# The last expert pass of a hybrid decoder block: its 128 places summed, normed and stored by index, and all tokens' rows stored under its products

## The chip, the cores and the metric

The kernel runs on one core of a Trainium2 chip. The metric is device time in microseconds (us) of one execution; a lower number is better. Three runs of the kernel before took 749.69, 751.23 and 755.02 us, so its median is 751.23 us. The profiled execution is a run of its own. It took 751.85 us, of which 750.1 us lie between its first and its last instruction (the span); the other 1.75 us lie outside.

A core has five engines with instruction streams of their own: PE (matrix products), DVE (vector), ACT (scalar functions), POOL and SP (here it only starts transfers). Each works through its stream in order and waits on semaphores.

## The reference, cut to what matters

One layer: a token mixer, then a mixture of experts, each in a residual branch, and a last RMS norm. There are 512 tokens of 1024 features. The change touches only how the experts' results are added to `x` and how the last norm and the output are made.

```python
def rms_norm(x, w):
    y = x * lax.rsqrt(jnp.mean(x * x, axis=-1, keepdims=True) + EPS)
    return y * w

def hier_moe(h, ...):            # 512 tokens, 32 experts, each token uses 2 experts of one group
    ...                          # comb[t, group, expert]: the two weights of a token, else 0
    for gi in range(N_GROUPS):
        a = silu(t @ w_e_gate[gi]) * (t @ w_e_up[gi])
        y = y + einsum('tef,te,efd->td', a, comb[:, gi], w_e_down[gi])
    return y

x = x + g1 * token_mixer(...)
h = rms_norm(x, norm2_w) * (1 + sc2) + sh2
x = x + g2 * hier_moe(h, ...)
return rms_norm(x, final_norm_w)
```

## The kernel before, in words

The experts are computed in 13 passes (`PASSES`, numbers 0 to 12; `NP` is 13). A pass has 128 **places**, shared out among two or four experts. The last pass has four experts (26 to 29) with 32 places each. A place holds one token of its expert, or is empty. `meta[:, 1]` is the place's token number, and `idx` the same as an integer. An empty place has a number of 512 or more, so that a transfer by index skips it.

One pass does this:

1. `up` multiplies the places' rows by the gate and up weights into the bank `gu`, in eight blocks `k`; blocks 0 to 3 use one set of weight tiles, blocks 4 to 7 another. With four experts each block is four products of 32 columns, which stand in four column groups of the PE array and can run beside each other. Between the two halves PE does the `add`s of the pass before (below).
2. ACT takes the silu of the gate half (line 1749), DVE multiplies it by the up half and the place's weight (`gate`, line 1754), PE turns the result (`turn`, line 1762) and ACT copies it out (line 1763).
3. `down` multiplies by the experts' down weights into two banks, one for each half of the features, and DVE scales them by g2 into `yf` (line 1784). In the last pass the products of the last expert, whose weights come last, stand behind those of the other three.
4. `add` returns the places' rows to their tokens: a 0/1 matrix `oht` (places by tokens) times `yf`, as a high and a low part (`yhi` from ACT, line 1785; `ylo` from DVE, line 1786), for 8 pieces of 128 tokens by 512 features. DVE adds each piece to `acc`, where the tokens' rows of `x` lie (line 1800).

After the last pass there is no later pass to hide the adds, so the kernel before does them another way. `total` (line 1429) puts each of the 8 pieces of `acc` into a bank with a product by the identity; these 8 products stand in the last pass where PE has gaps. After `down`, `add` adds the last pass's rows on top in the same banks (lines 1797, 1798). Then, token block by token block, ACT squares and sums the row (`squares`, line 1434), DVE makes the inverse root (`rsqrt`, lines 154 to 157, with a root on ACT, line 153), DVE, ACT and POOL scale by it and by the norm's weight (`finish`, lines 1449 to 1452) and SP stores the block of 128 rows (line 1453). Behind that, ACT and DVE copy all 8 banks back to `acc` (lines 1499, 1501), because `rest`, the program for tokens that don't fit into the places, would need them there; with this input no token is left over, and `rest` is branched past.

In the last pass `warm` also issues 12 and 8 small products by the identity, ahead of each half of `up` (line 1735, which calls line 215); nothing uses their results.

The order on PE and SP is that of the program text: each `step` holds its instructions behind the PE and SP instructions of the step before. The weights come as tiles of 1 MB through SP's queue (`load`, lines 974 and 976); the transfer of a tile waits for the eighth transfer before it to have landed, by one of eight semaphores in turn, and for its buffer to be free.

## Time and profile before

| | us |
|---|---|
| median of three runs | 751.23 |
| the profiled execution | 751.85 |
| its span | 750.1 |
| PE, DVE, ACT, POOL busy | 710.3, 510.5, 283.2, 91.3 |

The last passes and the end, by stretches of the span:

| stretch, us | what | PE busy | DVE busy | ACT busy | GB/s |
|---|---|---|---|---|---|
| 690.0 to 701.2 | pass 11 | 11.18 | 7.44 | 2.16 | 418 |
| 701.2 to 712.3 | pass 12, first half of `up`, adds of pass 11 | 11.15 | 5.09 | 2.23 | 419 |
| 712.3 to 730.7 | pass 12, second half of `up`, `down` | 18.37 | 3.33 | 2.88 | 222 |
| 730.7 to 750.1 | adds of pass 12, norm, stores, copies | 6.16 | 13.32 | 10.18 | 111 |

Up to 730.7 PE is busy all the time by this table, but it counts the small products of `warm` and the products by the identity too. So whether PE sets the pace in a stretch is read from what starts when, not from the share. From 730.7 on it is DVE and ACT, and then the last store.

### The profile page before, as it was taken

The numbers are of one execution on the slowest core, as the hardware profiler recorded it, in microseconds if no ns is written. First come the engines' busy times: TensorE is split into PE (matmuls) and PEld (weight loads), VectorE is DVE, ScalarE is ACT, GpSimd is POOL, SyncE is SP. The second block draws the span as 40 slices with busy tenths as digits, with TensorE's granted clock in tenths as the row PEclk, the third lists the DMA queues.
The fourth block names the chain that finished last, engine by engine and source line by source line (L and its number), as shares of the span: only waits on it lengthen the run. The fifth ranks groups of instructions, "written<-read, shape, count | busy, mean of one in ns | idle before, by whom it ended". The sixth has DMA issues, their size and how long they took to land.

```text
span 750.1 us, 11135 instructions
## 1 busy us (share of the span) xinstructions
PE 710.3 (95%) x4000; PEld 487.8 (65%) x4000; DVE 510.5 (68%) x1247; ACT 283.2 (38%) x548; POOL 91.3 (12%) x72
## 2 busy tenths in 40 slices
PE   7789999999998989999999999999999999999992
PEld 6567768878786868886768877884444444444631
DVE  5997678978646666768867744277776677766516
ACT  4345436852233212556753233224222322222215
POOL 1863000320222200000000000010100000000002
PEclk9999999999999999999999999999999999999997
DMA  9833223028787741361147997267999999999952
GB/s 360 301 129 115 84 88 108 30 66 297 240 279 244 240 165 57 99 239 49 58 148 283 342 422 291 78 254 261 403 408 403 403 411 411 410 412 419 419 211 114
DMA packets 47373, 182.89 MB, mean 244 GB/s; under 512 B 11717, under 2 KB 13285, under 8 KB 33875
## 3 DMA queue, kind: packets, MB, share of 16 engines
q1 hardware_dynamic: 40690, 169.91, 60.4%
q10 hardware_dynamic: 4896, 8.25, 3.0%
q0 software_dynamic: 1728, 3.99, 1.4%
q8 instruction: 32, 0.52, 0.3%
q14 instruction: 27, 0.21, 0.1%
HBM read 175.63 MB, written 8.80 MB: 246 GB/s over the span
## 4 chain that ended last, share of the span: by engine, by line
PE 71%; DVE 13%; DMA 8%; ACT 4%; issue 3%; POOL 0%; SPq 0%; DVEq 0%; ACTq 0%; POOLq 0%
PE gu L1726 12%; PE pj L139 9%; PE pj L141 9%; PE pj L140 9%; PE cb L1780 7%; DMA sgF<-w_mod 6%; PE cb L1797 3%; PE cb L1798 3%; DVE sF L220 3%; DVE sgF L220 2%; PE ax L801 2%; PE tr L1647 2%; DVE uS L145 1%; DMA aF<-rl 1%; DVE sh L315 1%
## 5 line engine op out<-in xcount | busy, mean ns | idle before, releaser
L139 PE MATMUL pj<-hR,uR 128*128 128x512 f32 x304 | 121.9, 401 | 1.5 <-DVE qk L737 1.5
L141 PE MATMUL pj<-hR,uS 128*128 128x512 f32 x304 | 122.1, 401 | 1.1 <-DVE uS L145 1.1
L140 PE MATMUL pj<-hR,uR 128*128 128x512 f32 x304 | 121.5, 400 | 0.0
L144 ACT ACTIVATE uR<-uF 128x1024 fp32r<-128x1024 f32 x48 | 50.8, 1059 | 92.3 <-PE pj L140 81.5
L145 DVE TENSOR_TENSOR uS<-uF,uR 128x1024 fp32r<-128x1024 f32 x48 | 59.7, 1243 | 24.6 <-ACT uR L144 24.2
L1800 DVE TENSOR_TENSOR accF<-accF,cb 128x512 f32<-128x512 f32 x96 | 60.3, 681 | 22.2 <-PE cb L1798 21.1
L1726 PE MATMUL gu<-ra,uS 128*64 128x512 f32 (+1 forms) x344 | 70.0, 597 | 0.0
L141 PEld LDWEIGHTS pj<-hR,uS 128*128 128x128 f32 x304 | 57.6, 189 | 13.4 <-DVE uS L145 3.2
L139 PEld LDWEIGHTS pj<-hR,uR 128*128 128x128 f32 x304 | 57.4, 189 | 12.5 <-issue 2.7
L140 PEld LDWEIGHTS pj<-hR,uR 128*128 128x128 f32 x304 | 57.5, 189 | 10.5 <-issue 0.3
L220 DVE SCALAR_TENSOR_TENSOR sgF<-sgF,misc 128x1024 f32<-128x1024 f32 x32 | 39.5, 1239 | 20.2 <-DMA sgF<-w_mod 19.9
L1726 PEld LDWEIGHTS gu<-ra,uS 128*64 128x64 f32 (+1 forms) x344 | 19.3, 123 | 36.4 <-issue 35.6
L1797 PE MATMUL cb<-uR,oht 128*128 128x512 f32 x100 | 42.6, 426 | 0.0
L1785 ACT ACTIVATE uR<-p2F 128x512 fp32r<-128x512 f32 x26 | 16.3, 630 | 65.9 <-DVE p2F L1784 65.9
L1749 ACT ACTIVATE uS<-gu 128x256 f32<-128x256 f32 x13 | 5.0, 384 | 95.7 <-PE gu L1726 95.7
L1798 PE MATMUL cb<-uR,oht 128*128 128x512 f32 x100 | 39.5, 395 | 0.1
L1780 PE MATMUL cb<-ra,uS 128*32 128x512 f32 (+1 forms) x160 | 38.3, 597 | 0.1
L1612 POOL DMA_INDIRECT uF<-xd,idx x12 | 12.4, 1036 | 180.1 <-PE tr L1647 121.6
L1754 DVE SCALAR_TENSOR_TENSOR uS<-uS,meta,gu 128x256 f32<-128x256 f32 x13 | 6.2, 481 | 37.1 <-ACT uS L1749 37.1
L1726 PE MATMUL gu<-rb,uS 128*32 128x512 f32 (+1 forms) x184 | 29.1, 595 | 0.0
L1784 DVE TENSOR_TENSOR p2F<-cb,p2F 128x512 f32<-128x512 f32 x26 | 17.8, 687 | 15.6 <-PE cb L1780 15.6
L220 DVE SCALAR_TENSOR_TENSOR sF<-sF,misc 128x1024 f32<-128x1024 f32 x16 | 27.7, 1740 | 0.2 <-DMA sF<-w_mod 0.2
(455 smaller groups left out, 1500.0 us busy)
## 6 DMA issues: line engine op xcount, KB each, us to landing
ra<-w_e SPq DMA_DIRECT2D x55, 1024.0 KB, 9.3
rb<-w_e SPq DMA_DIRECT2D x25, 1024.0 KB, 10.0
uF<-w_in SPq DMA_DIRECT2D x38, 512.0 KB, 3.5
sgF<-w_mod SPq DMA_DIRECT2D x32, 512.0 KB, 4.5
rc<-w_e SPq DMA_DIRECT2D x15, 1024.0 KB, 9.7
sF<-w_mod SPq DMA_DIRECT2D x8, 1024.0 KB, 9.5
gd<-sgF ACTq DMA_DIRECT2D x16, 256.0 KB, 3.6
gF<-gd SPq DMA_DIRECT2D x8, 512.0 KB, 3.6
```

The lines of the kernel that those rows point to most:

```text
L139: mm(ps, whi, xhi, start=first, stop=False)
L140: mm(ps, whi, xlo, start=False, stop=False)
L141: mm(ps, wlo, xhi, start=False, stop=last)
L144: self.nc.scalar.activation(hi, raw, AF.Copy)
L145: self.nc.vector.tensor_sub(lo, raw, hi.bitcast(F32))
L220: self.nc.vector.scalar_tensor_tensor(raw, raw, 1.0, self.cact, op0=OP.mult, op1=OP.mult, accum_out=self.mod[:, ot:ot + 1])
L1726: nc.tensor.matmul(gu[r], xe[:, k, r], w[:, k % 4], start=k == 0, stop=k == 7)
L1780: nc.tensor.matmul(dn[h][r], aT[:, f, r], w[:, f, c], start=f == 0, stop=f == 1)
L1784: v.tensor_mul(self.yf[:, c], dn[h], self.g2r[:, c])
L1797: nc.tensor.matmul(pc, self.oht[:, ts], self.yhi[:, c], start=own, stop=False)
L1798: nc.tensor.matmul(pc, self.oht[:, ts], self.ylo[:, c], start=False, stop=True)
L1800: nc.vector.tensor_add(self.acc[:, t, c], self.acc[:, t, c], pc)
```

## The change

The last pass's rows no longer go back to all 512 tokens. Instead:

- `alike` makes `same`, a 128 by 128 matrix that has a 1 where two places hold the same token, and a float copy `ohf` of the pass's matrix of tokens by places.
- `gather(h)` multiplies the tokens' rows in `acc` (with passes 0 to 11 added) by `ohf` into one bank for each half of the features: 4 products each. The bank then holds, for each place, its token's row. `gather(0)` stands between the halves of `up`, `gather(1)` behind `up`.
- All 512 tokens' rows are normed and stored during the last pass as they are then: `squares` on ACT, `roots` on DVE and ACT, `finish(0)` ahead of `gate` on DVE, `finish(1)` to `finish(3)` behind it; POOL no longer takes part. Tokens that have no place in the last pass are finished by that.
- After `down`, `finish_last` adds `same` times `yf` to the gathered rows (one product for each half), ACT squares and sums, DVE multiplies by the norm's weight, `store_last` makes the inverse root, scales the rows on ACT and DVE and stores the 128 rows by index, over those stored before. POOL issues this store, and waits for the four plain stores first.
- `warm` in the last pass, `total`, the 8 last adds, their high and low part, and the copies back are gone. The adds that `rest` needs stand inside its branch.

```diff
@@ moe: the last pass
             if p == NP - 1:
                 self.step(self.finish_init)
+                with ExitStack() as late:
+                    for x in self.after_down:
+                        late.enter_context(tc.issue_after(x))
+                    self.step(self.alike, p)
             self.up(p, p > 0, between=self.first_steps if p == 0 else None)
...
-                with tc.issue_after(self.sil.ins):
-                    nc.scalar.activation(self.rs[:, 0:1], self.ones[:, 0:1], AF.Sqrt)
+                self.step(self.gather, 1)
...
+            self.step(self.turn, p)
             if p == NP - 1:
-                self.dns = [self.bank() for _ in range(2)]
-                self.totals(2)
-            self.step(self.turn, p)
+                with tc.issue_after(self.gated.ins):
+                    for t in range(1, 4):
+                        self.finish(t)
+                with tc.issue_after(self.turned.ins):
+                    nc.scalar.activation(self.nt[:, 0:1], self.ones[:, 0:1], AF.Sqrt)
...
+            self.step(self.down, p, PASSES[p])
             if p == NP - 1:
-                self.totals(2)
-            self.step(self.down, p, PASSES[p])
+                for h in range(2):
+                    self.step(self.finish_last, h)
+                self.store_last(p)
...
-        for n in range(8):
...
-            self.step(self.add, n, self.fin[n])
-            self.squares(t, h, self.fin[n])
-            if h:
-                self.finish(t, (self.fin[n - 1], self.fin[n]))
@@ up
-            if p == NP - 1 and k % 4 == 0:
-                self.step(self.warm, self.bank(), self.ident, WL[k // 4])
             self.step(block, k)
...
             if p == NP - 1:
                 if k == 3:
                     for n in range(8):
                         self.step(self.add, n)
-                    self.totals(1)
+                    self.step(self.gather, 0)
+                    for ts in ((0, 1), (2, 3)):
+                        self.squares(ts)
+                        self.roots(ts)
+                    self.finish(0)
@@ new functions
+    def alike(self, p):
+        nc, tok = self.nc, self.meta[p % 4][:, 1:2]
+        nc.scalar.activation(self.ohf, self.oh[p % 2].rearrange("p t s -> p (t s)"), AF.Copy)
+        pr = self.tr.tile([128, 512], F32, name="tr")
+        nc.tensor.transpose(pr[:, 0:128], tok.to_broadcast([128, 128]), self.ident)
+        nc.vector.tensor_scalar(self.same, pr[:, 0:128], tok, None, op0=OP.is_equal)
+    def gather(self, h):
+        g = self.fin[h] = self.bank()
+        for t in range(4):
+            self.nc.tensor.matmul(g, self.ohf[:, 128 * t:128 * t + 128], self.half(2 * t + h), start=t == 0, stop=False)
+    def finish(self, t):
+        o = self.rows_out[t]
+        for h in range(2):
+            self.nc.vector.scalar_tensor_tensor(o[:, 512 * h:512 * h + 512], self.half(2 * t + h), self.rs[:, t:t + 1],
+                                                self.fw[:, 512 * h:512 * h + 512], op0=OP.mult, op1=OP.mult)
+        self.nc.sync.dma_start(self.out[t * 128:(t + 1) * 128], o)
+    def finish_last(self, h):
+        nc, v, o = self.nc, self.nc.vector, self.ends
+        c = slice(512 * h, 512 * h + 512)
+        s, g = self.ss[:, h, 4:5], self.fin[h]
+        nc.tensor.matmul(g, self.same, self.yf[:, c], start=False, stop=True)
+        nc.scalar.activation(self.sqj[2 + h], g, AF.Square, accum_out=s)
+        v.tensor_mul(o[:, c], g, self.fw[:, c])
+        if h == 0:
+            v.tensor_scalar(s, s, 1.0 / D, EPS, op0=OP.mult, op1=OP.add)
+    def store_last(self, p):
...
+        nc.scalar.activation(rs, s1, AF.Sqrt, scale=1.0 / D, bias=s0)
+        v.scalar_tensor_tensor(s1, s1, 1.0 / D, s0, op0=OP.mult, op1=OP.add)
+        self.rsqrt(rs, s1, "4", self.nt[:, 4:5], root=False)
+        nc.scalar.activation(o[:, 0:512], o[:, 0:512], AF.Copy, scale=rs)
+        v.tensor_scalar(o[:, 512:], o[:, 512:], rs, None, op0=OP.mult)
+        nc.gpsimd.indirect_dma_start(out=self.out, out_offset=bass.IndirectOffsetOnAxis(ap=self.idx[p % 4][:, :1], axis=0),
+                                     in_=o, in_offset=None, bounds_check=511, oob_is_err=False)
```

Where the instructions stand now, at three places. First PE between the two halves of `up` of the last pass. `cb` and `gu` are banks, `uR` the high and low rows, `ct` the identity, `rc` and `ra` weight tiles, and `rb_3430` holds `ohf`. Before, and then with the change:

```order
L1797 MATMUL cb<-uR,oht 128x512
L1798 MATMUL cb<-uR,oht 128x512
L1429 MATMUL gu<-accF,ct 128x512
L215 MATMUL cb<-ct 128x128 x8
L1726 MATMUL gu<-rc_3929,uS 32x512
L1726 MATMUL gu<-rc_3928,uS 32x512
```

```order
L1822 MATMUL cb<-uR,oht 128x512
L1823 MATMUL cb<-uR,oht 128x512
L1434 MATMUL cb<-accF,rb_3430 128x512 x4
L1750 MATMUL gu<-rc_3929,uS 32x512
L1750 MATMUL gu<-rc_3928,uS 32x512
```

One product by the identity and 8 small ones are replaced with the 4 products of `gather(0)`.

Second, PE in `down` of the last pass, from its second row on (`ra_3102` to `ra_3104` are the down weights of the first three experts, `rb_3427` those of the last). Before, and then with the change:

```order
L1780 MATMUL cb<-ra_3103,uS 32x512
L1780 MATMUL cb<-ra_3102,uS 32x512
L1780 MATMUL cb<-ra_3103,uS 32x512
L1429 MATMUL gu<-accF,ct 128x512
L1780 MATMUL cb<-ra_3104,uS 32x512
L1780 MATMUL cb<-ra_3102,uS 32x512
L1780 MATMUL cb<-ra_3103,uS 32x512
L1780 MATMUL cb<-ra_3104,uS 32x512 x2
L1780 MATMUL cb<-ra_3102,uS 32x512
L1780 MATMUL cb<-ra_3103,uS 32x512
L1780 MATMUL cb<-ra_3104,uS 32x512
L1780 MATMUL cb<-rb_3427,uS 32x512 x4
```

```order
L1807 MATMUL cb<-ra_3103,uS 32x512
L1807 MATMUL cb<-ra_3102,uS 32x512
L1807 MATMUL cb<-ra_3104,uS 32x512
L1807 MATMUL cb<-ra_3102,uS 32x512
L1807 MATMUL cb<-ra_3103,uS 32x512
L1807 MATMUL cb<-ra_3104,uS 32x512
L1807 MATMUL cb<-ra_3103,uS 32x512
L1807 MATMUL cb<-ra_3104,uS 32x512
L1807 MATMUL cb<-ra_3102,uS 32x512
L1807 MATMUL cb<-ra_3103,uS 32x512
L1807 MATMUL cb<-ra_3104,uS 32x512
L1807 MATMUL cb<-rb_3427,uS 32x512 x4
```

The product by the identity no longer stands between the third expert's products and those of the first two.

Third, ACT from the start of the last pass to its last row (line 1441 is `squares`, 152 the root, 1775 the silu, 1789 the copy of `turn`, 1465 to 1477 the end). With the change:

```order
L1425 ACTIVATE rb_3430<-uS 128x512
L1441 ACTIVATE rb_3431,ss_5991<-accF 128x512 x8
L152 ACT_TABLE_LOAD
L152 ACTIVATE rs_5992<-ss_5991 128x2 x2
L1775 ACT_TABLE_LOAD
L1775 ACTIVATE uS<-gu 128x256
L1789 ACTIVATE uS<-tr 128x256
L1388 ACT_TABLE_LOAD
L1388 ACTIVATE nt_5993<-ct 128x1
L1465 ACTIVATE rb_3431,ss_5991<-cb 128x512 x2
L1474 ACTIVATE rs_5992<-ss_5991 128x1
L1477 ACTIVATE rb_3430<-rb_3430,rs_5992 128x512
```

Before, the silu (line 1749) was ACT's first instruction of the pass behind the copies of line 1464, and one table load stood behind it; now 8 squares, two roots and two table loads stand ahead of it, and one load behind the copy of `turn`.

## Rows read from the trace of the kernel before

**Rows 1.** Timeline, PE, last pass: start us, length us, engine, line, operation, count.

```profile
704.88 0.63 PE L1726 MATMUL gu<-ra,uS 128*32 128x512 f32 x3
...
712.33 1.02 PE L1429 MATMUL gu<-accF,ct 128*128 128x512 f32 x2
713.18 1.95 PE L215 MATMUL cb<-ct 128*128 128x128 f32 x16
715.06 0.62 PE L1726 MATMUL gu<-rc,uS 128*32 128x512 f32 x2
...
718.63 1.98 PE L1429 MATMUL cb<-accF,ct 128*128 128x512 f32 x4
720.45 0.38 PE L1762 MATMUL tr<-ct,uS 128*128 128x128 f32 x2
...
722.48 1.91 PE L1780 MATMUL cb<-ra,uS 128*32 128x512 f32 x8
```

**Rows 2.** Timeline, PE, further on in `down` of the last pass.

```profile
725.38 2.33 PE L1780 MATMUL cb<-ra,uS 128*32 128x512 f32 x13
727.13 0.62 PE L1780 MATMUL cb<-rb,uS 128*32 128x512 f32 x1
...
728.41 0.59 PE L1780 MATMUL cb<-ra,uS 128*32 128x512 f32 x1
```

**Rows 3.** Timeline, SP's queue: weights of `down`'s last expert, then the last store.

```profile
704.28 2.97 SPq L974 DMA_DIRECT2D rb<-w_e  x2
...
744.53 0.33 SPq L1453 DMA_DIRECT2D out<-rb  x1
```

**Rows 4.** Chain that ended last, its last piece: start us, us, what.

```profile
744.42 2.47 DVE accF L1499 x4
```

**Rows 5.** Timeline, ACT, last pass.

```profile
718.77 0.38 ACT L1749 ACTIVATE uS<-gu 128x256 f32<-128x256 f32 x1 [15.30 <-PE gu L1726]
719.17 1.28 ACT L1370 ACT_TABLE_LOAD   x1
...
720.93 0.38 ACT L1763 ACTIVATE uS<-tr 128x256 f32<-128x256 f32 x1 [0.26 <-PE tr L1762]
```

**Rows 6.** Timeline, DVE, last pass and what follows it.

```profile
709.22 4.87 DVE L1800 TENSOR_TENSOR accF<-accF,cb 128x512 f32<-128x512 f32 x8 [5.51 <-PE cb L1798]
...
730.78 0.69 DVE L1784 TENSOR_TENSOR p2F<-cb,p2F 128x512 f32<-128x512 f32 x1 [1.02 <-PE cb L1780]
```

**Rows 7.** Groups from 730.7 on: busy us, mean ns of one, idle before.

```profile
L155 DVE TENSOR_TENSOR nt<-ss,rs 128x1 f32<-128x1 f32 x4 | 2.7, 680 | 0.1
L1434 ACT ACTIVATE rb<-cb 128x512 f32<-128x512 f32 x4 | 2.3, 588 | 0.2 <-PE cb L1798 0.2
...
L1434 ACT ACTIVATION_READ_ACCUMULATOR rb<-cb 128x1 f32 x4 | 0.8, 199 | 0.0
...
L1449 ACT ACTIVATE rb<-cb,rs 128x512 f32<-128x512 f32 x1 | 0.7, 688 | 0.2 <-DVE rs L157 0.2
...
L157 DVE SCALAR_TENSOR_TENSOR rs<-nt,rs 128x1 f32<-128x1 f32 x4 | 0.6, 159 | 0.1
```

**Rows 8.** The fetches by index, line 1612, of 504 to 510 us: issue to landing.

```profile
DMA to landing us min/median/max: 3.9/4.1/4.2
```

**Rows 9.** The same line over the whole span.

```profile
DMA to landing us min/median/max: 3.9/8.1/8.9
```

**Rows 10.** The plain stores, line 1453.

```profile
DMA to landing us min/median/max: 2.6/3.0/3.3
```

**Rows 11.** Timeline, PE: a break of 1.49 us ahead of 161.31 us.

```profile
161.31 0.47 PE L139 MATMUL pj<-hR,uR 128*128 128x512 f32 x1 [1.49 <-DVE qk L737]
```

**Rows 12.** Two stretches: busy of five engines, then granted clock, DMA share, GB/s.

```profile
161.00:164.00 3.00, 2.69 (x12) 2.25 (x13) 2.91 (x5) 1.12 (x3) 0.85 (x1) 1.00 0.31 34
...
268.00:272.00 4.00, 4.00 (x19) 3.42 (x18) 3.07 (x7) 0.64 (x1) 0.00 (x0) 0.60 0.56 168
```

**Rows 13.** The page's DMA queue of the fetches by index: packets, MB, share of 16 engines.

```profile
q0 software_dynamic: 1728, 3.99, 1.4%
```

## What the change does to the time: the prediction

> **What bounds the kernel now.** The stretches of the table say where to look: up to 730.7 us PE never rests, behind it DVE and ACT work and PE hardly does. The change lies behind 701 us, so I read that stretch engine by engine on the timeline, then took prices from the groups.
>
> In the last pass two things set PE's pace. One is the weights: SP could start the first half of the last expert's tile only at 704.28 [rows 3], when the eighth transfer before it, the fourth expert's tile of the first half of `up`, had landed; that half started at 704.88 [rows 1], right behind the small products of `warm`. The two transfers of line 974 span 2.97 us [rows 3], the second one's own 0.4 included, so a tile takes some 2.6 us. The fourth tile of the second half comes four tiles later, near 714.7; that half started at 715.06 [rows 1]. So the small products stand where PE would wait anyway. The other is PE's own work: from 715.06 on each of its pieces starts where the one before ends.
>
> Behind PE's last `down` product, at 730.78 by DVE's start [rows 6], the end is a chain: adds, squares, roots, scalings, and the last store, issued at 744.53 [rows 3]. Stores land after 2.6 to 3.3 us [rows 10]. The chain of waits itself ends with DVE's copies, at 746.9 [rows 4], but the store issued at 744.53 lands near 747.8, later than these, so taking the copies away alone would give nothing.
>
> **The change, part by part.** I follow one moment, E, at which `down` is done (730.78 now), then the way from E to the last store, then the rest.
>
> *First half of `up`.* Without 12 small products PE is ready near 702.5, but the fourth tile lands at 704.28. So it starts at 704.3 instead of 704.88: **-0.6**. `alike` (a copy of the kind of ACT's 0.6 us, a small transpose, a comparison) fits into that wait.
>
> *Between the halves.* From 712.33 to 715.06 [rows 1] one product by the identity and 8 small ones took 2.73 us. Two products of that form take 1.82 us (718.63 to 720.45), so one is 0.9 and `gather(0)` 3.6: **+0.9**. Its last product needs DVE's seventh add; eight adds take 4.87 us from 709.22 [rows 6], so that is done near 713, before PE asks. The second half starts at 715.3, later than its weights.
>
> *Behind `up`.* From 718.63 to 722.48 PE ran four products by the identity and the transposes. The gathers take the same 3.6 us, but nothing now hides ACT's copy: the transposes start at 720.45 and the copy ends at 721.31 [rows 1, 5], so 0.9 follow: 4.5 instead of 3.85, **+0.65**. This assumes silu and `gate` done within these 3.6 us. ACT's 8 squares follow DVE's adds and end near 714.5; a load (1.28 [rows 5]), two roots and another load end near 717.5, and the silu is due at 719.0. DVE's eight small operations and `finish(0)`, two of 0.61 to 0.75 us, end near 719 too, ahead of `gate` at 719.4. So they are hidden with 1.5 us on ACT, and with hardly any on DVE.
>
> *`down`.* It took 8.3 us. With its product by the identity gone, the last expert's four products, one behind the other in their column group, decide. In [rows 2] they start at 727.13, 1.75 us after 725.38, when in each group two products were done, although the third expert's last product, which the program places ahead of them, starts only near 728. So a group's next product waits in line without stopping the other groups. In the new order the last expert can then start two products (1.75) after `down` starts, and needs 727.13 to 730.78, 3.65 us: 5.4 in all, **-2.9**. Its weights are there: by 2.6 us a tile near 724 and 725, and their second half is wanted near 727.
>
> E comes at 730.8 - 0.6 + 0.9 + 0.65 - 2.9 = 728.85: **-1.95**.
>
> *From E to the last store.* Now 744.53 - 730.78 = 13.75. Then: 0.69 for g2 [rows 6], the second `same` product 1.1 behind it (one such product is 1.02 to 1.13 alone), a square with its sum 0.6 and 0.2 partly beside each other, 0.7 [rows 7], DVE's product with the norm's weight, which waits for the square, 0.7, five small operations at 0.16 [rows 7] and their gaps, 0.85, ACT's scaling 0.69 [rows 7], and 0.1 for semaphores: 4.85. The root lies beside DVE's product. Line 155 took 680 ns on the mean [rows 7] while POOL multiplied; POOL no longer does, so I take 160. **-8.9**. The four plain stores, queued behind the weights to 725, need 2 MB at some 400 GB/s and land near 731, before the 733.7 at which POOL wants to store.
>
> *From the store to the end.* Now 750.1 - 744.53 = 5.6 us, 3.3 of them the landing. No store by index is in this trace. Its nearest rows are the fetches by index of the same 128 rows: 3.9 to 4.2 us while the queue of weights was quiet [rows 8], 8.1 on the median, mostly beside it [rows 9]; the plain store's 2.6 [rows 10] is the bound below. The weights are over by then, so I take 4.1: **+0.8**; the ends are -0.7 and +4.8. The Trainium skill's page "DMA: Bandwidth & Descriptors", section "Anatomy of one DMA — SWDGE (gpsimd) path", gives 2.0 us and the bytes at 436 GB/s, by which these 0.5 MB would land after 3.2 and the sum would be 0.9 lower (an estimate); the quiet fetches took more, and I keep theirs.
>
> Removed at no gain: the copies back and the low and high parts (the latter lay in the chain now counted from E).
>
> The sum is -1.95 - 8.9 + 0.8 = **-10.05**. Against the profiled 751.85 that is 741.8; the median of the runs shown stands 0.6 below, so I forecast 741.2.
>
> **The rivals.**
>
> *Column groups in strict order.* If a product that waits for its group stops all behind it, the new order lets the last expert start only after four steps, 3.5 us, and E comes at 730.6: 1.75 later, 743.0. [Rows 2] speak against it. The Trainium skill's page "TensorE: Matmul & The Clock Gate", section "Part 3: Packing small matmuls — row/col tiling", says so: matmuls start and end in program order. The trace disagrees where the last expert's first row (727.13) stands ahead of the third's last (728.41). Chance 0.1.
>
> *The store by index lands as late as the fetches did beside the weights,* 6 to 9 us instead of 4.1: 743.1 to 746.1, mostly within 1%. For it: nothing here shows a write by index. Against: what made them late by the trace, the stream of weights, is over. Chance 0.13.
>
> *The clock falls.* Without the small products PE rests some 0.8 us near 703.5 and 0.9 before `down`. Against: behind 1.49 us of rest the granted clock stayed 1.00, the 2.4 GHz level [rows 11, 12]. A fall like that near 268 us, where 4 us ran at 0.60 on the mean [rows 12], partly at 1.2 GHz, would cost 1.6: 742.8, two of them 744.4. Chance 0.06.
>
> *Slower: the store by index goes through one transfer engine.* The queue of the fetches moved 3.99 MB, 974 rows of 4 KB, with 1.4% of 16 engines' span, 168 us, so 0.17 us a row [rows 13]. Spread over 16 engines 128 rows take 1.4 us, through one 22, and the landing is 24.7: 761.8. It decides from a landing of about 14 us, that is, from two engines down. Against: fetches of the same 128 rows and index landed within 4.2, so theirs were spread. Chance 0.03. That `rest` is entered after all, which would also show the change not doing what it says, I leave in the last few per cent: nothing of it ran before, and its condition is unchanged.
>
> **The numbers.** The forecast as summed, 739 to 743.5, has 0.65; strict order 0.1, the late store 0.13, the clock 0.06, slower 0.03, and other troubles 0.03 (within 1%). From 743.7 on the result counts as no change: 1% is about what a measurement of this kernel can tell. Faster: the forecast, most of strict order and a few hundredths of the two others, 0.80; within 1% 0.16; slower 0.04. The low end takes the plain store's landing (-1.5) and the runs' spread (1), 738.7; the high end strict order together with part of the late store, 745.7.
>
> **What would show it.** In the changed profile: the first half of `up` at 704.3 behind a wait for weights; the second at 715.3; `down` from 723.4 with the last expert's first product some 1.75 us later, E near 728.9; POOL's store at 733.7 with a landing near 4 us, the end at 740. I am wrong if the silu comes late behind its table load, if `gate` waits for `finish(0)`, if the last expert starts 3.5 us into `down`, or if POOL's store starts when a plain store lands and not when the scaling ends.

## The result and the profile after

The changed kernel takes **742.72 us** in the median of 5 runs (741.91 to 745.42); the kernel before took 751.23 (749.69 to 755.02). The ratio is 0.9887, with a 95% interval of 0.9851 to 0.9922: 8.5 us less, and surely less. The forecast was 741.2, in a range of 738.7 to 745.7. The profiled execution after took 742.16 us, with a span of 740.0.

Nothing ahead of the last pass was changed, yet in the 14 traces of this study that pass's first product (the transposes of `spread`) starts anywhere between 698.9 and 706.2 us. A difference of a few us in the total is therefore read by stages, each from its own start. Before and after:

| stage of the last pass | before, us | after, us | forecast | measured |
|---|---|---|---|---|
| up to `spread` (unchanged) | 701.18 | 701.89 | 0 | +0.71 |
| to the end of the adds | 11.15 | 10.49 | -0.6 | -0.66 |
| to the second half of `up` | 2.73 | 3.60 | +0.9 | +0.87 |
| second half of `up` | 3.57 | 3.57 | 0 | 0 |
| to the start of `down` | 3.85 | 4.39 | +0.65 | +0.54 |
| `down`, to E | 8.30 | 5.44 | -2.9 | -2.86 |
| E to the start of the last store | 13.75 | 5.40 | -8.9 | -8.35 |
| from there to the end | 5.6 | 5.2 | +0.8 | -0.35 |

From `spread` on the sum is -10.8, against -10.05 forecast. The second row needs care, because with the change PE waits there for weights. SP's next transfer waits for the same landing as the fourth expert's first product: after, they start at 704.80 and 704.83. In the ten traces without the small products (the changed kernel and the versions of it below) that landing came 1.8 to 3.3 us behind `spread`, and the stage took 9.34 to 10.86 us. Before, it came 3.10 behind (704.28), nearly as late as after (2.91), so these two executions can be compared, but the -0.66 is not a fixed length.

```profile
704.80 2.96 SPq L973 DMA_DIRECT2D rb<-w_e  x2
```

Here is PE's timeline after, whose starts answer to [rows 1, 2] (start, length, engine, line, operation, tiles, count, idle before and who ended it; a gather's four products count x8, two records each):

```profile
701.89 1.09 PE L1489 MATMUL tr<-ct,c_cols 128*128 128x128 f32 x8
...
704.83 0.62 PE L1750 MATMUL gu<-rc,uS 128*32 128x512 f32 x1 [0.29 <-DMA rc<-w_e]
...
712.38 3.67 PE L1434 MATMUL cb<-accF,rb 128*128 128x512 f32 x8
715.98 0.62 PE L1750 MATMUL gu<-rc,uS 128*32 128x512 f32 x2
...
719.55 3.70 PE L1434 MATMUL cb<-accF,rb 128*128 128x512 f32 x8
723.09 0.38 PE L1788 MATMUL tr<-ct,uS 128*128 128x128 f32 x2
...
723.94 2.37 PE L1807 MATMUL cb<-ra,uS 128*32 128x512 f32 x15 [0.47 <-ACT uS L1789]
725.72 0.62 PE L1807 MATMUL cb<-rb,uS 128*32 128x512 f32 x1
726.11 0.63 PE L1807 MATMUL cb<-ra,uS 128*32 128x512 f32 x3
```

The fourth expert's products wait for their weights, as the prediction said; each gather takes 3.7 us; in `down` the last expert (`rb`) starts 1.78 us behind the first product, where 1.75 was forecast. `down` is done when DVE takes its second half, at 729.38. The way from there to the end, all engines in one timeline:

```profile
729.38 0.69 DVE L1809 TENSOR_TENSOR p2F<-cb,p2F 128x512 f32<-128x512 f32 x1 [1.01 <-PE cb L1807]
...
731.29 0.60 ACT L1465 ACTIVATE rb<-cb 128x512 f32<-128x512 f32 x1 [0.17 <-PE cb L1464]
...
732.01 0.69 DVE L1466 TENSOR_TENSOR rb<-cb,uF 128x512 f32<-128x512 f32 x1
...
733.46 0.72 ACT L1477 ACTIVATE rb<-rb,rs 128x512 f32<-128x512 f32 x1 [1.15 <-DVE rs L156]
733.46 0.48 DVE L1478 TENSOR_SCALAR rb<-rb,rs 128x512 f32<-128x512 f32 x1
734.78 1.01 POOL L1479 DMA_INDIRECT out<-rb,idx  x1 [66.36 <-DVEq L1522]
```

A reader should see the last line. The scalings end at 733.94 (DVE) and 734.18 (ACT), and POOL's store starts only at 734.78. Its landing, by the DMA issues:

```profile
out<-rb,idx POOLq DMA_INDIRECT x1, 3.3
```

It lands 3.3 us after its issue, like the plain stores of [rows 10]; in the other eight traces with the same store below it is 3.2 to 3.7. It moves less than the forecast had counted: the queue of transfers by index moved 4.23 MB, where it was 3.99 [rows 13], so 0.24 MB, some 59 of the 128 rows; the other places are empty. The clock held, by the view of the stretches that answers to [rows 12] (the granted clock is the figure behind the five engines):

```profile
712.30:728.90 16.60, 16.13 (x83) 5.62 (x82) 9.55 (x25) 7.74 (x18) 0.00 (x0) 1.00 0.94 379
```

### The profile page after: what moved, and what is told of

The parts are those of the page before. It is cut to its first block, busy times and chain, and to the rows that moved or that the text cites. A ratio compares the mean times of both kernels' runs of the same rounds, so it can differ in the third digit from the quotient of the medians.

```text
span 740.0 us, 11015 instructions
## 1 busy us (share of the span) xinstructions
PE 707.5 (96%) x3949; PEld 482.3 (65%) x3949; DVE 507.3 (69%) x1241; ACT 283.2 (38%) x546; POOL 88.2 (12%) x70
## 3 DMA queue, kind: packets, MB, share of 16 engines
q0 software_dynamic: 1872, 4.23, 1.5%
## 5 line engine op out<-in xcount | busy, mean ns | idle before, releaser
L140 PEld LDWEIGHTS pj<-hR,uS 128*128 128x128 f32 x304 | 57.3, 189 | 12.6 <-DVE uS L144 1.3
L1822 PE MATMUL cb<-uR,oht 128*128 128x512 f32 x96 | 41.1, 428 | 0.0
L1823 PE MATMUL cb<-uR,oht 128*128 128x512 f32 x96 | 37.8, 394 | 0.0
L1807 PE MATMUL cb<-ra,uS 128*32 128x512 f32 (+1 forms) x160 | 36.5, 597 | 0.6 <-ACT uS L1789 0.5
L138 PE MATMUL pj<-mR,uR 128*128 128x512 f32 (+1 forms) x72 | 27.3, 379 | 0.0
```

The source lines that it names most:

```text
L138: mm(ps, whi, xhi, start=first, stop=False)
L140: mm(ps, wlo, xhi, start=False, stop=last)
L1807: nc.tensor.matmul(dn[h][r], aT[:, f, r], w[:, f, c], start=f == 0, stop=f == 1)
L1822: nc.tensor.matmul(pc, self.oht[:, ts], self.yhi[:, c], start=True, stop=False)
L1823: nc.tensor.matmul(pc, self.oht[:, ts], self.ylo[:, c], start=False, stop=True)
```

## The experiments

**Are the copies behind the last store on the path?** The kernel before, with only this edit (the tiles' last readers stay, with a 512th of the work):

```
- nc.vector.tensor_copy(half(i), self.fin[i])
- nc.scalar.activation(half(i), self.fin[i], AF.Copy)
+ nc.vector.tensor_copy(half(i)[:, 0:1], self.fin[i][:, 0:1])
+ nc.scalar.activation(half(i)[:, 0:1], self.fin[i][:, 0:1], AF.Copy)
```

> The kernel before, with the eight copies behind the last store cut to one column each (the branch that would read the rest never runs here). Theory: the copies end before the last store has landed and are on no path that sets the end, so 751.2 within 1 us, and the end still 5.6 us behind the issue of the last store. Rival: the chain of waits ended with these copies, so the end follows them; they run 2.5 us on DVE, and without them the time would be 748.7.

Measured: ratio to before 0.9993 (0.9976 to 1.0009), 750.3 us. The chain of waits ended with these copies [rows 4], and cutting them gave nothing that can be told: the last store is issued at 742.24, 13.76 behind E (728.48), where it was 13.75, and the end comes 5.4 us later, where it was 5.6. So no part of the gain that can be told comes from leaving the copies out.

**Did POOL slow DVE's small operations?** Again the kernel before, with `nc.gpsimd.tensor_tensor` of `finish` made `v.tensor_tensor`.

> The kernel before, with POOL's three multiplications in the last rows' norm given to DVE. Theory: line 155 took 680 ns on the mean because POOL multiplied at that moment; without that it takes 160, which gives 2.1 us over four, and DVE's three products of 0.7 us take 2.1 again: 751.2 within 1 us, line 155 at 160 ns. Rival: line 155 is slow for another reason (what it reads): it stays near 680, and the three products come on top, 753.3.

Measured: ratio 0.9987 (0.9964 to 1.001), 749.85 us, no change that can be told by the time. The groups of the tail (busy us, mean ns), and where the tail starts and its last store:

```profile
L1450 DVE TENSOR_TENSOR rb<-rb,uF 128x512 f32<-128x512 f32 x3 | 2.1, 693 | 0.2 <-ACT rb L1449 0.2
L155 DVE TENSOR_TENSOR nt<-ss,rs 128x1 f32<-128x1 f32 x4 | 0.6, 157 | 0.0
```
```profile
730.55 0.69 DVE L1784 TENSOR_TENSOR p2F<-cb,p2F 128x512 f32<-128x512 f32 x1 [1.02 <-PE cb L1780]
...
736.90 6.57 SPq L1453 DMA_DIRECT2D out<-rb  x4
```

Line 155 went from 680 to 157 ns, as the theory had it. By its stage the edit did gain: the last store is issued at 743.14 (the four issues end at 743.47, the last takes 0.33), 12.6 us behind E (730.55), where the kernel before took 13.75. So taking POOL out of the old tail alone is worth 1.2 us. In the trace of the kernel before, line 155's three long instances end with POOL's multiplication beside them; two of them in the timeline:

```profile
736.46 1.27 POOL L1450 TENSOR_TENSOR rb<-rb,uF 128x512 f32<-128x512 f32 x1 [68.70 <-ACT rs L153]
736.50 0.16 DVE L154 RECIPROCAL rs<-rs 128x1 f32<-128x1 f32 x1
736.70 1.05 DVE L155 TENSOR_TENSOR nt<-ss,rs 128x1 f32<-128x1 f32 x1
...
738.93 1.26 POOL L1450 TENSOR_TENSOR rb<-rb,uF 128x512 f32<-128x512 f32 x1 [1.20 <-ACT rb L1449]
739.45 0.76 DVE L155 TENSOR_TENSOR nt<-ss,rs 128x1 f32<-128x1 f32 x1
```

A product of one column waited until POOL was through (737.75 and 737.73; 740.21 and 740.19), while the reciprocal at 736.50, which reads one operand, ran beside POOL in 0.16. The Trainium skill's page "SBUF — State Buffer", section "SBUF: two separate sides", says that a DVE operation with two inputs in SBUF and a GpSimd operation that reads SBUF lock each other out for a whole instruction; the trace agrees, with 1.05 and 0.76 us instead of 0.16. The prediction's 160 ns for this line in the new chain rests on that.

**Is it the product by the identity that made `down` long?** The changed kernel, with it put back behind the fourth of the 16 products:

```
+            if p == NP - 1 and t == todo[3]:
+                with self.tc.issue_after(i.ins):
+                    self.more = nc.tensor.matmul(self.gu.tile([128, 512], F32, name="gu"), self.ident, self.half(7),
+                                                 start=True, stop=True)
...
```

> The changed kernel, with one product by the identity back inside the last pass's products of the third weight part, behind the fourth of them, as before the change. Theory (the term of -2.9): a product over the whole array parts the work of the column groups, so 1.84 for four products, 1.06 for it, and then as long as the changed kernel takes in all: these products take 8.3 instead of 5.44 us, their end comes at 732.3 instead of 729.4, and the time is 745.6. Rival: it costs only its own time, 1.06 at most, or runs in a gap: 743.8 or 742.7.

```profile
724.69 1.90 PE L1810 MATMUL cb<-ra,uS 128*32 128x512 f32 x8 [0.47 <-ACT uS L1789]
726.53 1.12 PE L1813 MATMUL gu<-accF,ct 128*128 128x512 f32 x2
727.58 1.48 PE L1810 MATMUL cb<-ra,uS 128*32 128x512 f32 x8
728.48 0.62 PE L1810 MATMUL cb<-rb,uS 128*32 128x512 f32 x1
```

Measured: 744.46 us (ratio to before 0.9918, 0.9891 to 0.9944). `down` takes 7.44 us (724.69 to DVE's 732.13) instead of 5.44: **2.0 of the 2.9**. The 1.84 ahead of it and its own 1.05 came as expected; behind it the last expert starts after 0.9 us, not 1.75 as in [rows 2]. The other 0.9 is put down to the order; this run does not vary it by itself. In the kernel before, the four products ahead belonged to two experts, and all four of the third stood behind it; here all three had begun. One rule fits these starts: products are handed out in order, one may wait for its column group behind the one that runs there, and the next for that group stops everything behind it. Before, by the instruction lists shown ahead, all four products of `ra_3104` stood between the identity and the last expert, which so had to wait for two of them (1.75); here at most three of each stood there, and it waited for one (0.9); in the changed kernel, with four of each ahead, for two again (1.78). The other orders below fit the rule too.

**What does the cover give?** The changed kernel, with the squares, roots, products and stores of the 512 rows placed in the code behind the last `same` product:

```
-                with tc.issue_after(self.gated.ins):
-                    for t in range(1, 4):
-                        self.finish(t)
...
                 for h in range(2):
                     self.step(self.finish_last, h)
+                self.squares(range(4))
+                self.roots(range(4))
+                for t in range(4):
+                    self.finish(t)
                 self.store_last(p)
...
-                    for ts in ((0, 1), (2, 3)):
-                        self.squares(ts)
-                        self.roots(ts)
-                    self.finish(0)
```

> The changed kernel, with the squares, roots, products and plain stores of all 512 rows moved behind the second square of the last 128 rows. Theory: the 8.9 us came from the cover that the last pass's products give to this work, so without it ACT takes 8 squares of 0.61, DVE some 1 us of small operations and 8 products of 0.75, the last plain store lands 3 us later and only then the store by index starts: near 747 instead of 734.8, and the time is 754.6, 12 us more and above the kernel before. Rival: most of the 8.9 came from summing and norming in 128 places (no adds, no copies back); then this work costs what DVE alone needs, 6 us, 748.7 or less.

Measured: 746.47 us (ratio to before 0.9941, 0.992 to 0.9963). The expectation misjudged the edit: ACT's squares wait only for the adds and still ran under `up`, from 712.6 to 717.6 us. DVE's part of the roots stopped at 719.37 and went on at 728.16, behind an ACT instruction that writes the same tile `nt` and stands ahead of it in the code (line 1385 here). So only DVE's eight products and the four stores came late, between the last steps. The timeline of SP's queue, DVE and POOL:

```profile
730.19 7.38 SPq L1458 DMA_DIRECT2D out<-rb  x4
...
737.97 0.49 DVE L1479 TENSOR_SCALAR rb<-rb,rs 128x512 f32<-128x512 f32 x1
...
741.08 1.01 POOL L1480 DMA_INDIRECT out<-rb,idx  x1 [69.98 <-SPq L1523]
```

E is at 732.10 here, POOL's store 8.98 later, against 5.40. Two things show: DVE's last scaling comes at 737.97 instead of 4.1 behind E, at 736.2; and the store then waits for the last plain store, whose issue ends at 737.57, 3.5 ahead. So the cover for these products and stores, as far as this run takes it away, is worth 3.6 us. Of the other 4.8 of the 8.35, POOL's leaving the tail gave 1.2 where it was tried alone. How the rest divides between the squares' cover and the 128 places in place of 512 rows, no run here tells apart.

**Does the order of `down` still cost?** The changed kernel without `todo.sort(...)`, the line that puts the last expert's products behind the other twelve.

> The changed kernel, with the last expert's four products of the third part no longer placed behind the other twelve. Theory, from the starts in the two traces and in a_ident: products are handed out in order, one may wait for its column group while another runs there, and the next for that group stops all behind it; so the last expert started 1.78 us late only because its products stand last. In mixed order it starts with the others, all four groups need 4 products of 0.87, the products end 3.6 instead of 5.44 us behind their start, at 727.5, and the time is 740.9. Rival: its weights land only near 725, which is why the order was so; then its first product waits in front and stops the others behind it: the end stays at 729.4 or comes later, 742.7 or more.

```profile
720.00 3.70 PE L1434 MATMUL cb<-accF,rb 128*128 128x512 f32 x8
...
724.39 1.07 PE L1804 MATMUL cb<-ra,uS 128*32 128x512 f32 x6 [0.47 <-ACT uS L1789]
724.94 0.62 PE L1804 MATMUL cb<-rb,uS 128*32 128x512 f32 x1
```

Measured: `down` takes 4.21 instead of 5.44 (to DVE's 728.60); 741.33 us (ratio to before 0.9877, 0.9855 to 0.99). That is two thirds of the expected 1.85, because the last expert starts 0.55 behind the first. The rule gives 0 for the seventh place in the order, and the weights account for the 0.55: by the trace's record of landings the last piece of this expert's first tile lands at 724.90, and its product starts at 724.94. (The profile shows no wait there, since PE has other products to do.) In the changed kernel the same tile had landed at 723.47, 2.25 ahead of the product. So theory and rival each hold in part.

**What does the uncovered copy cost?** Three of the second gather's four products moved behind the transposes:

```
- self.step(self.gather, 1)
+ self.step(self.gather, 1, range(1))
...
  self.step(self.turn, p)
+ self.step(self.gather, 1, range(1, 4))
```

> The changed kernel, with three of the four products of the second gather moved behind the transposes, so that PE has work while ACT copies them. Theory (the term of +0.65, of which 0.9 was the copy with nothing to hide it): the wait of 0.47 and the end of the transposes before it go, the products of the third part start 0.85 us earlier, at 723.1, and so does their end, 728.5: 741.9. Rival: the last expert's weights, not PE, set the moment 725.72 at which it starts; then the end stays at 729.4, 742.7. Second rival: the transposes now wait for the silu and the gate's product, which end near 720.5: at most 0.2 of the gain is lost.

```profile
720.39 1.12 PE L1435 MATMUL cb<-accF,rb 128*128 128x512 f32 x2
721.48 0.44 PE L1789 MATMUL tr<-ct,uS 128*128 128x128 f32 x2
721.75 2.74 PE L1435 MATMUL cb<-accF,rb 128*128 128x512 f32 x6
724.43 2.35 PE L1808 MATMUL cb<-ra,uS 128*32 128x512 f32 x15
```

Measured: from the gather's start to `down` 4.04 instead of 4.39, 0.35 gained, not 0.85: of the 0.85 between the transposes' start and `down` 0.38 are the transposes themselves, and PE has to do them anyway. At most the idle 0.47 was there to be had. 742.63 us (ratio 0.9885, 0.9855 to 0.9916).

**What are the 0.6 us ahead of POOL's store?** The changed kernel, with this behind the plain stores:

```
+ for t in range(4):
+     nc.gpsimd.memset(self.rows_out[t][:, 0:1], 0.0)
```

> The changed kernel, with POOL writing one column of each of the four plain stores' sources before the end, so that POOL has waited for these stores long before the store by index. Theory for the 0.6 us between the last scaling's end (734.18) and POOL's start (734.78): POOL goes through the waits for the stores and for DVE and ACT one by one, and most of it goes: the store starts 0.3 to 0.5 us earlier behind the scaling, 742.3. Rival: the 0.6 us is what a store by index needs to start on POOL behind any wait; nothing changes, 742.7.

```profile
732.37 0.10 POOL L1388 MEMSET rb<- 128x1 f32 x1 [0.92 <-SPq L1524]
737.37 1.01 POOL L1481 DMA_INDIRECT out<-rb,idx  x1 [4.90 <-DVEq L1524]
```

Measured: the rival. POOL had waited for the four stores by 732.37, and its store still starts 0.6 behind ACT's scaling (736.76) and 0.84 behind DVE's (736.53). The waits for the stores are free; 743.0 us (0.9894, 0.9855 to 0.9933).

What the time is counted from, POOL's own waits show (count, shortest, median and longest in ns, first and last start in us). The first row is the changed kernel, the second the run with the late products:

```profile
L1479 POOLq EVENT_SEMAPHORE  x3: 43/43/4277, 727.2 to 729.7; - x3
...
L1480 POOLq EVENT_SEMAPHORE  x3: 42/43/43, 734.8 to 740.2; - x3
```

In the changed kernel the last wait starts at 729.71 and ends at 733.99, with DVE's scaling; the store starts 0.80 later. In the run with the late products the last wait is for a plain store and ends at 740.28, when DVE's and ACT's scalings had been over for 1.8 and 1.6 us; the store starts at 741.08, 0.79 later. So the store starts 0.8 us behind POOL's last wait, whatever that waits for (0.79 or 0.80 in all ten traces with a store by index). The releaser that the timeline names, DVE's line 1522, is a branch behind the scaling and does not fit: in the late run that branch was over more than 1 us ahead of the store. What POOL does in the 0.80 us, no run shows.

**All together, and the tail's small operations first.** The three edits above, and DVE's second product with the norm's weight taken together with its scaling, behind the root:

```
- v.tensor_mul(o[:, c], g, self.fw[:, c])
+ if h == 0: v.tensor_mul(o[:, c], g, self.fw[:, c])
- v.tensor_scalar(o[:, 512:], o[:, 512:], rs, None, op0=OP.mult)
+ v.scalar_tensor_tensor(o[:, 512:], self.fin[1], rs, self.fw[:, 512:], op0=OP.mult, op1=OP.mult)
```

> The changed kernel with the three edits together (mixed order of the last products, three products of the second gather behind the transposes, POOL's waits taken early), and the second half's product with the norm's weight taken by DVE together with the scaling, behind the root, so that the small operations need not wait for it. Theory: -1.85, -0.85, -0.4 and -0.3 add up to -3.4: 739.3. Rival: the weights of the last expert land near 725 and take back the first two: 741.9. Second rival: POOL then waits for the plain stores, which landed at 729.7 at the latest: by the theory it wants to store near 731.3, so this decides only if they land 1.6 us later than before.

```profile
727.44 0.69 DVE L1809 TENSOR_TENSOR p2F<-cb,p2F 128x512 f32<-128x512 f32 x1 [0.76 <-PE cb L1807]
...
731.25 0.75 DVE L1481 SCALAR_TENSOR_TENSOR rb<-cb,rs,uF 128x512 f32<-128x512 f32 x1
...
732.84 1.01 POOL L1482 DMA_INDIRECT out<-rb,idx  x1 [2.67 <-DVEq L1525]
```

Measured: 741.29 us (0.9883, 0.9857 to 0.9909), not 739.3. From the second gather's start (719.10) E comes after 8.34 us where it was 9.83: -1.49, about the sum of the two edits as measured (1.23 and 0.35). The tail gained nothing: the scalings start 3.81 behind E instead of 4.08, but DVE's takes 0.75 instead of 0.48, and POOL starts 0.84 behind DVE's end, as in the changed kernel (733.94 to 734.78), so 5.40 again. Here ACT ends at 731.97, 0.87 ahead of POOL's start, where that was 0.60 in the changed kernel; POOL's last wait, for DVE, ends 0.80 ahead in both. The last expert starts 0.64 behind the first (723.78 and 723.14), again 0.04 behind the landing of its weights (723.74).

**The last expert first.** The split gather, and the order of `down` in rounds of four, the last expert ahead (`lead` is its product in the round):

```
- todo.sort(key=lambda t: t[2][0] == len(ps) - 1)
+ todo.sort(key=lambda t: (t[0], t[1], t[2][0] != len(ps) - 1))
...
+                if p == NP - 1 and lead:
+                    es.enter_context(self.tc.issue_after(lead.ins))
```

> The changed kernel with three products of the second gather behind the transposes, and the last pass's products of the third part in rounds of four, the last expert's ahead of the other three in each. Theory: in the mixed order the last expert started 0.55 us late because it stood seventh; first in the order it starts with the rest, and the four groups need 4 products of 0.87 each: from the second gather's start to the end of these products 7.7 us, where the changed kernel took 9.83, mixed order 8.60 and mixed order with the split gather 8.34; the time 740.6. Rival: its weights have not landed at 723, and as the first in the order it stops all: 8.3 us or more, 741.3 or more.

```profile
722.02 1.12 PE L1435 MATMUL cb<-accF,rb 128*128 128x512 f32 x2
...
726.79 0.59 PE L1812 MATMUL cb<-rb,uS 128*32 128x512 f32 x1 [0.67 <-DMA rb<-w_e]
726.80 0.63 PE L1812 MATMUL cb<-ra,uS 128*32 128x512 f32 x3
```

Measured: both theories have their part. All four groups start together and `down` takes 3.70 (to 730.49); but it starts 0.67 late, behind the last expert's weights. From the gather's start 8.47 us; without that wait 7.8, as expected. 741.74 us (0.988, 0.9856 to 0.9904). The expectation's reason, the seventh place, was wrong (the weights made the 0.55, as said above), and its rival's reason was right. With PE's own waits gone, the weights hold the last expert back: in this version, in that with all edits and in that with mixed order its first tile lands 4.6 to 4.9 us behind the second gather's start. None of these versions can be told from the changed kernel by its time; the lowest median, 741.29, is 1.4 us below it.

**What did the small products cost?** The changed kernel with them back:

```
+ if p == NP - 1 and k == 0:
+     self.step(self.warm, self.bank(), self.ident, 12)
+ if p == NP - 1 and k == 4:
+     self.step(self.warm, self.tr.tile([128, 512], F32, name="tr"), self.ident, 8)
```

> The changed kernel with the 12 and 8 small products back ahead of the two halves of the last pass's up projection. Theory (the terms -0.6 and +0.9): the 12 fill most of a wait for weights and move the first half's end by 0.6 us (6.49 us from the spread transposes to the adds become 7.1); the 8 run where nothing is waited for and cost their 1.8 us whole: 745.1. The granted clock stays 1.00 in both kernels from 701 to 729 us. Rival: they keep the clock up, and without them PE ran slower somewhere in the last pass: then they cost less than 2.4, and some stretch is faster with them.

```profile
702.56 1.09 PE L1489 MATMUL tr<-ct,c_cols 128*128 128x128 f32 x8
...
704.06 2.84 PE L214 MATMUL cb<-ct 128*128 128x128 f32 x24
714.39 3.67 PE L1434 MATMUL cb<-accF,rb 128*128 128x512 f32 x8
717.90 1.95 PE L214 MATMUL tr<-ct 128*128 128x128 f32 x16
```
```profile
701.00:729.00 28.00, 27.27 (x172) 14.21 (x167) 15.10 (x35) 12.71 (x28) 0.00 (x0) 1.00 0.93 383
```

Measured: 745.94 us (0.9951, 0.993 to 0.9971), 3.2 more than the changed kernel by the medians. The 8 cost 1.80 as expected (714.39 to the second half's 719.79, 5.40 instead of 3.60). With the 12 the stage to the gather takes 11.83 instead of 10.49, 1.34 more and twice the 0.6. They now stand behind `alike`'s transpose, which waits for ACT, and end near 706.9, when the weights have long landed. But the weights came early in this execution: SP's next transfer, which shows their landing, is at 704.23, 1.7 behind `spread`, where it was 2.9 in the changed kernel. In the two versions with a landing at 1.8 and 1.9 and without the 12 the stage took 9.34 and 9.42. Against the ten traces without them the 12 cost 1.0 to 2.5 us: the earlier the weights land, the more. The granted clock is 1.00 with them and without.

**What sets the landing?** The store by index with 128 different rows as its index; its rows land in the wrong places.

> The changed kernel, with the store by index given 128 different rows 0 to 127 instead of the tokens of the 128 places, most of which are empty (0.24 MB moved, some 59 rows). What it computes is no longer the reference's: the rows land in the wrong places. Theory: 3.3 us of landing instead of the 4.1 forecast came from the empty places; with all 128 rows it lands after 4.1, as the fetches did, 743.5. Rival: the landing does not depend on the number of rows (the packets spread over 16 engines): 3.3 and 742.7.

```profile
out<-rb,pli POOLq DMA_INDIRECT x1, 3.4
```

Measured: the rival. The queue moved 0.52 MB for this store, and the landing is 3.4 us, within the 3.2 to 3.7 of the nine traces with 0.24 MB. The empty places did not make it fast; the fetches were the wrong neighbour. The time, 744.43 (0.9923, 0.9902 to 0.9944), does not show that: in the profiled run the last pass starts at 706.21, 4.3 us later than in the changed kernel's, and POOL's store is 5.41 behind E as ever. Why its runs were longer ahead of that, nothing here shows.

**And against a plain store?** A plain store from SP in its place, again to the wrong rows:

```
- nc.gpsimd.indirect_dma_start(out=self.out, ..., in_=o, ...)
+ nc.sync.dma_start(self.out[0:128], o)
```

> The changed kernel, with the store by index replaced by a plain store of the same 128 rows from SP to rows 0 to 127; the rows land in the wrong places. Theory (the term +0.8, of 1.3 by what the end now shows): a plain store is issued 0.1 us behind the last scaling instead of 0.6 to 0.84, and lands after 2.6 to 3.3: from the end of the scalings to the end 5.6 us, as before the change, instead of 5.8: 742.5. Rival: storing by index costs POOL's start and its microsecond of preparing on top: then the plain store ends 1.5 us or more earlier, 741.2.

```profile
732.93 0.33 SPq L1479 DMA_DIRECT2D out<-rb  x1
```

Measured: SP issues it 0.03 behind the last scaling's end (732.90), and the end comes 5.4 us behind that (738.3), against 5.8 by index (734.18 to 740.0): storing by index costs 0.4 us in all; 741.73 (0.9893, 0.9872 to 0.9915).

## Why the prediction was right

- **First half of `up`, -0.6:** -0.66, behind a wait for weights. The mechanism was right: the small products stood where PE would wait. The size holds for these two executions, in which the weights landed 3.10 and 2.91 us behind `spread`; in ten traces the stage took 9.34 to 10.86, where the kernel before had 11.15.
- **Between the halves, +0.9:** +0.87.
- **Behind `up`, +0.65:** +0.54. Silu and `gate` were in time: ACT sat idle 1.85 us ahead of the silu, and `gate` waited for it, not for `finish(0)`.
- **`down`, -2.9:** -2.86, with the last expert 1.78 behind the first product. The mechanism was half named: the product by the identity accounts for 2.0, and the other 0.9 is put down to the order of the others around it. The prediction let a group's next product wait without stopping the other groups; the starts fit that for one waiting product of a group only, and it was the second that held the last expert back (1.75 and 1.78). Strict order, the first rival, is out: it would have put the last expert 3.5 us into `down`. The Trainium skill's page "TensorE: Matmul & The Clock Gate", section "Part 3: Packing small matmuls — row/col tiling", has matmuls start and end in program order; the trace after disagrees as that of before did, with `rb` at 725.72 ahead of products of `ra` that stand before it.
- **E to the store, -8.9:** -8.35. The term that was mis-sized is the start of the store: 0.1 was put down for semaphores behind ACT's scaling, and POOL's store starts 0.80 behind its last wait, which ends with DVE's scaling, 0.2 ahead of ACT's: 0.6 behind ACT's. The chain before that took 4.8 to the end of ACT's scaling, as summed.
- **Store to end, +0.8:** -0.35, the one term with the wrong sign. The landing is 3.3, not 4.1, with 59 rows as with 128; the plain store's row was the better neighbour, and the rest behind the landing is 1.9 where 2.3 had been. The Trainium skill's page "DMA: Bandwidth & Descriptors", section "Anatomy of one DMA — SWDGE (gpsimd) path", by which the estimate was 3.2 for 0.5 MB, was nearer to the 3.4 measured than the fetches' 4.1. For 0.24 MB the estimate by it is 2.6, and 3.2 to 3.7 were measured.
- **The rivals:** the late landing and the one transfer engine fall with 3.3 us; the fall of the clock with 1.00 up to 728.9; the copies that were called free were free.

The two errors behind E (+0.55 and -1.15) and those ahead of it (-0.16) leave -0.76; the unchanged part ahead came 0.71 later in this execution, and 0.4 more than before lies outside the span. (All five runs of the changed kernel have some 2.2 us there, the kernel before 1.8; why, no run shows.) So the profiled 742.16 stands nearer to its 741.8 than the terms do to theirs, and that is luck. The median stands 1.5 above the forecast, mostly because that of the runs after lies 0.56 above the profiled one, while before it lay 0.62 below.

## What to carry to other kernels

Take a kernel's end from its last step that needs the last data, and ask what of the work behind it needs them at all: here the norm of all rows but the last pass's own did not, and went under the products ahead. Where several small products share the array by columns, read the order in which they are handed out before costing them, and count as a gain from covering only the idle time, not the work beside it. A difference below 1% is settled by the lengths of the stages, since a part that nobody touched moved by up to 7 us between runs. A stage that begins with a wait for weights is measured from their landing. And where an engine has other work to do, look at the landing itself: the profile names no wait, though one product is held back.

## What had not been expected of the hardware

- A store by index of 0.24 MB landed after 3.2 to 3.7 us (nine traces), one of 0.52 MB after 3.4; fetches by the same kind of index after 3.9 to 4.2 [rows 8].
- POOL's store by index starts 0.80 us behind the end of POOL's last wait (0.79 or 0.80 in ten traces), whether that wait is for DVE or for a plain store. Behind the end of DVE's last operation that is 0.84.
- A product for a busy column group lets others pass while it is the only one to wait there; the second stops them. This fits the last expert's starts in all the orders tried: 1.75, 0.90 and 1.78 us behind the first, and with the three mixed orders 0.04 to 0.13 us behind the landing of its weights.
